# Summing the first half of the feed-forward shift on VectorE beside the output projection

## The chip, the cores and the metric

The kernel runs on one core of a Trainium2 chip. The metric is the device time of one execution in microseconds. The kernel before was run three times: 1297.34, 1301.3 and 1302.14 us, median 1301.3 us. Another execution was recorded by the hardware profiler; it took 1299.62 us, of which the profile's span covers 1297.8.

## The reference

One layer of a decoder with a batch of one, 256 tokens (T), width 2048 (D) and a feed-forward width of 5632, all in float32:

```python
cond = silu(c)
mod = (cond @ w_mod + b_mod).reshape(B, 6, D)
sh1, sc1, g1, sh2, sc2, g2 = [mod[:, i, None, :] for i in range(6)]
h = rmsnorm(x, norm_mix) * (1.0 + sc1) + sh1
proj = h @ w_in
...
y = concatenate([gla, gated_deltanet, pool, fox], -1) @ w_out
x = x + g1 * y
h = rmsnorm(x, norm_ffn) * (1.0 + sc2) + sh2
x = x + g2 * conv_ffn(h, w_gate, w_up, conv_w, conv_b, w_down)
return rmsnorm(x, norm_final)
```

The four mixers (gated linear attention, gated delta rule, pooling, forgetting attention) have 512 columns each. What the change concerns is `mod`: six vectors of 2048 numbers, each a product of the one vector `cond` with 2048 rows of `w_mod`. `sh2`, the shift ahead of the feed-forward part, is needed only after the output projection and the norm.

## The kernel before

**Stages.** By the trace: the input projection and the first two modulation vectors to about 240 us, then the rest of the input projection together with the four mixers, to about 448 us; the output projection to 541; the norm; the feed-forward part to the end. TensorE multiplies float32 weights as a sum of three products of rounded halves: ScalarE casts a loaded weight tile `wr` to its high half `wh`, VectorE takes the rest as `wl` (`load_split`, L158–163), and each k-row tile needs three matmuls of (`xh`,`wh`), (`xh`,`wl`), (`xl`,`wh`).

**The modulation gemvs.** The vectors that are needed later are made in halves of 1024 columns, in the background: a "job" is a letter and a half, `s0`, `s1` for the scale `sc2`, `h0`, `h1` for the shift `sh2`, `g0`, `g1` for the gate `g1`. A job (`gemv`, L171–206) goes through 16 rows of tiles of `w_mod`, two per step, each a transfer of 512 KB into a ring `wm` of four buffers, issued by SP. There are two ways to sum them.
- On TensorE (`ON_PE`): four matmuls of 32 columns by 512 for a row tile pair go side by side into four column strips of one PSUM bank `bgt`; at the end ScalarE copies the bank to a buffer `gr` of the `wr` ring, and eight matmuls with one column each (`sel`) add the strips and turn the row into a column, which VectorE adds to `s2` or `sh2` (`to_col`).
- On VectorE (`ON_DVE`): 16 scalar-tensor-tensor operations `ga <- wm, cond, ga` sum the rows within each partition; the end is matmuls with `ones`, eight of one column for a column vector (`to_col`) or two of 512 for a row (`to_row`, the `g` jobs).

**What sets the order.** The program is written as generators. While the last part of the input projection is emitted piece by piece, `paced` (L908) advances the two background streams by 0.38 and 0.69 of a step per piece; what is left of them is drained at L940–943. The `g` jobs wait with their end until the `s` jobs and the mixer whose buffer they reuse are emitted. A scheduler then orders the instructions of each engine by priority and by its own estimate of when each can run, so matmuls of one strand fill holes of another. Each engine works through its queue in that order; SP issues the transfers in its order too, and a transfer that waits for a buffer holds those behind it.

**The output projection.** `project(n, a)` (L952) goes through five chunks of columns (512, 512, 512, 256, 256) and, within one, through the 16 row tiles of `w_out` in the order of the mixers. A load is 512 KB: two row tiles of 512 columns or four of 256, so the chunks have 8, 8, 8, 4 and 4 loads. A load of two row tiles gives 12 matmuls of 512 columns (two row tiles, two halves of the tokens, three products), and chunk 0 has 96. Chunk 0 sums into the banks `ext`, chunk 1 into `oxt`, chunk 2 into `wot`, then `ext` and `oxt` again. Chunk 0 can run beside the end of the mixers as far as the mixers' results are there.

**The end of the mixers.** The delta rule (`gated_deltanet`) is a chain over four chunks of 64 tokens on banks `gdt`; its output is normed (`jk` squares on ScalarE, `oss` on VectorE and one power on POOL at L726, then `Y`), transposed (`gdt<-ident,Y`, L735) and multiplied into `pr`. The forgetting attention (`fox`) has four heads of two tiles: scores in `oxt` (last matmul `oxt<-ngr,idr`), maximum on VectorE (L868), exponent on ScalarE, reciprocal on VectorE (L870), scaling on ScalarE, one or two transposes (`oxt<-ident,p`, L873), a copy `pt` on ScalarE, and three matmuls with the values (`oxt<-pt,fv`). The results are split into the halves of `Y2` (in rows: `bigA<-pr`), which `project` multiplies. The tile `x1` (in rows `bigC`) takes x again for the residual sum, by two transfers of 1 MB (L979).

Of the kernel before, what the change touches and what calls it, by code (L numbers as in the profile page):

```python
# [49 lines left out]

ORDER = "gpfd"

ON_PE, PE_RATE = "s0 s1 h0", 0.38
ON_DVE, DVE_RATE = "h1 g0 g1", 0.69


def _consts():
# [16 lines left out]
def trunk_kernel(ctx: ExitStack, tc: tile.TileContext, x, c, w_mod, b_mod, norm_mix, norm_ffn, w_in,  # L74
# [21 lines left out]
    def mm(o, l, r, start=True, stop=True):  # L96
        PE.matmul(o, lhsT=l, rhs=r, start=start, stop=stop, skip_group_check=True)  # L97

    def tt(o, a, b, op):
        V.tensor_tensor(out=o, in0=a, in1=b, op=op)  # L100
# [10 lines left out]
    def act(o, a, f, **kw):  # L111
        S_.activation(o, a, f, **kw)

    def split(hi, lo, src):
        S_.copy(hi, src)  # L115
        tt(lo, src, hi.bitcast(F32), ALU.subtract)
# [36 lines left out]
    def load(view, k0, nk, c0, n):  # L153
        wr = wp.tile([P, 1024], F32, name="wr", tag="wr", bufs=5).rearrange("p (k n) -> p k n", n=n)
        nc.sync.dma_start(wr[:, 0:nk], view[:, k0:k0 + nk, c0:c0 + n])  # L155
        return wr

    def load_split(view, k0, nk, c0, n):  # L158
        wr = load(view, k0, nk, c0, n)
        wh = wp.tile([P, 1024], F32R, name="wh", tag="wh", bufs=3).rearrange("p (k n) -> p k n", n=n)  # L160
        wl = wp.tile([P, 1024], F32R, name="wl", tag="wl", bufs=3).rearrange("p (k n) -> p k n", n=n)
        split(wh[:, 0:nk], wl[:, 0:nk], wr[:, 0:nk])
        return wh, wl
# [51 lines left out]
    def to_col(dst, i, k0, nw, pst):  # L215
        def f(parts):
            b = pst()
            for j, (src, one) in enumerate(parts):
                for q in range(4):
                    mm(b[:, 4 * j + q:4 * j + q + 1], src[:, q * P:q * P + P], one[:, 0:1])  # L220
            o = dst[:, k0:k0 + 8]
            tt(o, b[:, 0:8], bm(i, k0, 8), ALU.add)
            if nw is not None:
                tt(o, o, nw[:, k0:k0 + 8], ALU.mult)
        return f


    with ExitStack() as ph:
# [16 lines left out]
        ext = lambda: exp_.tile([P, 512], F32, name="ext", tag="ext")  # L245
# [42 lines left out]
        with ExitStack() as st:  # L288
# [46 lines left out]
            def mods(g):  # L335
                for k0 in range(GROUPS[g][0], sum(GROUPS[g]), 4):
                    yield from mods4(k0, min(4, sum(GROUPS[g]) - k0))
# [135 lines left out]
                    yield from pair(p, done[p], g + 1)  # L473
                    done[p] = g + 1

            def jobs(seq, pst):
                col = pst or (ext)
                for job in seq.split():
                    kind, n = job[0], int(job[1])
                    k0, col0 = 8 * n, dict(s=4, h=3, g=2)[kind] * D + n * 1024  # L480
                    if kind == "s":
                        yield from gemv(col0, to_col(s2, 4, k0, nffn, col), pst)
                    elif kind == "h":
                        yield from gemv(col0, to_col(sh2, 3, k0, None, col), pst)
                    else:
                        yield from gemv(col0, g1_row(n, bgt), None,
                                        lambda: "gf"[n] in emitted and "s" in emitted, b_mod[:, col0:col0 + 1024])
# [3 lines left out]
            def marked(steps):  # L491
                yield from steps
                emitted.add("s")
# [4 lines left out]
            def g1_row(n, row):  # L498
                def f(parts):
                    name = ("gv", "fv")[n]  # L500
                    g1t[n] = cp.tile([P, 1024], F32, name=name, tag=name)
                    to_row(g1t[n], 0, row)(parts)
                return f

            bgt = lambda: bgp.tile([P, 512], F32, name="bgt", tag="bgt")
            bg = [marked(jobs(ON_PE, bgt)), jobs(ON_DVE, None)]
            for _ in mods(0):
                pass
            hold = [last_wm[0]]
# [437 lines left out]
        chunks = ((0, 512), (512, 512), (1024, 512), (1536, 256), (1792, 256))  # L947
        Y2 = bigA()

        def project(n, a):  # L950
            c0, w = chunks[n]
            nk = 1024 // w  # L952
            for j in range(KT // nk):
                ks = order[nk * j:nk * j + nk]
                if n == 0:
                    for k in ks:
                        split(Y2[:, k, 0:T], Y2[:, k, T:], pr[:, k + 4])
                wh, wl = load_split(wo_v, ks[0], nk, c0, w)
                steps = [(kk, k, t) for kk, k in enumerate(ks) for t in range(NT)]
                if n == len(chunks) - 1 and ks[-1] == order[-1]:  # L960

                    steps.sort(key=lambda s: s[2])
                for kk, k, t in steps:
                    st, sp_ = j + kk == 0, nk * j + kk == KT - 1
                    xh, xl = Y2[:, k, t * P:t * P + P], Y2[:, k, T + t * P:T + t * P + P]
                    mm(a[t], xh, wh[:, kk], start=st, stop=False)
                    mm(a[t], xh, wl[:, kk], start=False, stop=False)
                    mm(a[t], xl, wh[:, kk], start=False, stop=sp_)
# [3 lines left out]
        for n in range(2):  # L972
            project(n, sums[n])
# [7 lines left out]
        with tc.tile_pool(name="op", bufs=2, reuse_waits="tile") as op:  # L981
            for n, (c0, w) in enumerate(chunks):
                ns, gs = slice(c0, c0 + w), slice(c0 % 1024, c0 % 1024 + w)
                if n < 2:
                    a = sums[n]
                else:
                    a = [(wot, ext, oxt)[n - 2]()[:, 0:w] for _ in range(NT)]
                    project(n, a)
                for t in range(NT):
                    m_ = op.tile([P, 512], F32, name="m_", tag="m_")[:, 0:w]  # L990
                    tt(m_, a[t], g1t[c0 // 1024][:, gs], ALU.mult)
                    tt(x1[:, t, ns], x1[:, t, ns], m_, ALU.add)
                    act(m_, x1[:, t, ns], AF.Square, accum_out=x1s[:, t, n:n + 1])


    with ExitStack() as ph:
# [3 lines left out]
        with tc.tile_pool(name="hp", bufs=2, reuse_waits="tile") as hp:  # L1000
            s1 = hp.tile([P, 4], F32, name="s1", bufs=1)
# [145 lines left out]
```

## Time and profile before

| what | value |
|---|---|
| median of three runs | 1301.3 us (1297.34 to 1302.14) |
| profiled execution | 1299.62 us |
| its span in the profile | 1297.8 us |
| granted TensorE clock, mean | 0.985 |
| data moved over the span | 311.91 MB, mean 240 GB/s |
| matmuls `bgt<-wm,cond` (three jobs) | 192, 38.0 us busy |
| sums `ga<-wm,cond,ga` on VectorE | 139, 178.1 us busy, 1281 ns each |
| splits `wl<-wr,wh` on VectorE | 384, 469.4 us busy, 1223 ns each |

The profile is of one execution. It gives the busy time of each engine: PE is TensorE's matmuls, PEld its weight loads, DVE VectorE, ACT ScalarE, POOL GpSimd, SP the engine that issues the transfers. Rows of groups read: line, engine, operation, `out<-in`, shapes, count, then busy time, the mean of one in ns, and the idle time ahead of it with what ended that. Rows of the timeline begin with the start and the duration in us. PEclk is the TensorE clock that was granted, 1.00 being full speed. L97 is the line of a helper through which every matmul goes, so that groups are told apart by the names of tiles.

### The profile page before, as it was taken

Reading aid. Unit: us, or ns where it says so; the run is one execution under the profiler, and the core shown is the slowest. Engines: PE = TensorE matmul, PEld = TensorE weight load, DVE = VectorE, ACT = ScalarE, POOL = GpSimd, SP = SyncE. Lnnn points to the kernel's source line nnn. Section 1 sums busy time; section 2 is a strip of 40 time slices with the busy share of each in tenths; the row PEclk is TensorE's granted clock in tenths of the full one; section 3 lists DMA queues with packets and bytes.
Section 4 is the critical chain, followed back from the end, with each engine's and each line's share of the span. In section 5 each row is a group of like instructions: output and inputs, shape, how many; then the busy total and the mean of one; then the engine's idle time right before and its main releaser. Section 6 shows DMA issues by size and latency. Waiting matters only on the chain.

```text
span 1297.8 us, 19845 instructions
## 1 busy us (share of the span) xinstructions
PE 1243.1 (96%) x7663; PEld 1075.8 (83%) x7663; DVE 889.1 (69%) x1201; ACT 636.2 (49%) x1000; POOL 23.1 (2%) x31
## 2 busy tenths in 40 slices
PE   2799999999999999999999999999999999999995
PEld 1799999898876688888888888888888888888884
DVE  7679797989763397676657666665666587964543
ACT  3455344774354454564545545554545444443432
POOL 0200000010000100000000000000000000000000
PEclk9799999999999999999999999999999999999998
DMA  9899999796567898556576666657665699875552
GB/s 326 274 367 377 333 333 302 255 334 227 163 231 248 306 330 279 155 165 192 163 212 193 179 196 194 182 172 209 186 191 165 212 364 379 307 259 184 193 194 81
DMA packets 168597, 311.91 MB, mean 240 GB/s; under 512 B 16172, under 2 KB 54067, under 8 KB 167863
## 3 DMA queue, kind: packets, MB, share of 16 engines
q1 hardware_dynamic: 168503, 310.65, 73.0%
q8 instruction: 60, 0.98, 0.3%
q14 instruction: 34, 0.28, 0.1%
HBM read 308.51 MB, written 2.10 MB: 239 GB/s over the span
## 4 chain that ended last, share of the span: by engine, by line
PE 91%; DMA 4%; SPq 1%; DVE 1%; ACT 1%; issue 1%; POOLq 0%; ACTq 0%; DVEq 0%
PE fpt L97 57%; PE ext L97 16%; PE oxt L97 5%; PE acc L97 4%; PE gdt L97 4%; DMA wm<-in_w_mod_dram 3%; PE bgt L97 3%; PE wot L97 2%; DMA wr<-in_w_in_dram 1%; DVE ga L103 1%; ACT xT L1015 0%; SPq L155 0%; SPq L399 0%; DVE m L100 0%; DVE wl L100 0%
## 5 line engine op out<-in xcount | busy, mean ns | idle before, releaser
L100 DVE TENSOR_TENSOR wl<-wr,wh 128x1024 fp32r<-128x1024 f32 x384 | 469.4, 1223 | 293.7 <-ACT wh L115 292.9
L115 ACT CAST wh<-wr 128x1024 fp32r<-128x1024 f32 x384 | 403.6, 1051 | 489.5 <-PE fpt L97 316.5
L97 PE MATMUL fpt<-bigA,wh 128*128 128x512 f32 x1408 | 399.6, 396 | 2.1 <-DVE bigA L103 2.1
L97 PEld LDWEIGHTS fpt<-bigA,wh 128*128 128x128 f32 x1408 | 239.2, 189 | 32.9 <-issue 2.2
L97 PEld LDWEIGHTS fpt<-bigA,wl 128*128 128x128 f32 x1408 | 222.6, 188 | 34.2 <-DVE wl L100 3.7
L97 PE MATMUL fpt<-bigA,wl 128*128 128x256 f32 x1408 | 240.5, 279 | 0.0
L103 DVE SCALAR_TENSOR_TENSOR ga<-wm,cond,ga 128x1024 f32<-128x1024 f32 x139 | 178.1, 1281 | 11.5 <-DMA wm<-in_w_mod_dram 10.6
L97 PE MATMUL fpt<-wl,AH 128*128 128x512 f32 x352 | 137.5, 391 | 0.0
L97 PE MATMUL ext<-bigA,wh 128*128 128x256 f32 x768 | 137.3, 281 | 0.0
L97 PE MATMUL fpt<-wh,AL 128*128 128x512 f32 x352 | 137.0, 389 | 0.0
L97 PE MATMUL fpt<-wh,AH 128*128 128x512 f32 x352 | 123.5, 390 | 0.0
L97 PEld LDWEIGHTS ext<-bigA,wh 128*128 128x128 f32 x768 | 117.5, 189 | 3.0 <-DVE dS L100 0.8
L97 PE MATMUL ext<-bigA,wl 128*128 128x256 f32 x384 | 107.4, 280 | 1.7 <-DVE wl L100 1.7
L97 PE MATMUL ext<-wh,bigA 128*128 128x256 f32 (+1 forms) x384 | 79.3, 300 | 0.0
L97 PEld LDWEIGHTS fpt<-wh,AH 128*128 128x128 f32 x352 | 66.1, 188 | 14.1 <-ACT wh L115 0.2
L97 PEld LDWEIGHTS fpt<-wl,AH 128*128 128x128 f32 x352 | 66.1, 188 | 13.9 <-DVE m L100 0.2
L97 PEld LDWEIGHTS fpt<-wh,AL 128*128 128x128 f32 x352 | 66.1, 188 | 13.8 <-issue 0.2
L97 PE MATMUL acc<-bigA,wh 128*128 128x256 f32 x384 | 70.1, 289 | 4.6 <-ACT bigA L115 2.7
L97 PEld LDWEIGHTS ext<-bigA,wl 128*128 128x128 f32 x384 | 72.1, 188 | 2.8 <-DVE wl L100 1.9
L97 PEld LDWEIGHTS ext<-wh,bigA 128*128 128x128 f32 x384 | 61.6, 188 | 5.5 <-ACT wh L115 1.7
L97 PEld LDWEIGHTS acc<-bigA,wh 128*128 128x128 f32 x384 | 60.7, 199 | 5.0 <-ACT bigA L115 2.8
L97 PE MATMUL ext<-wl,bigA 128*128 128x256 f32 (+1 forms) x192 | 58.3, 304 | 1.6 <-DVE wl L100 1.6
(344 smaller groups left out, 1172.1 us busy)
## 6 DMA issues: line engine op xcount, KB each, us to landing
wm<-in_w_mod_dram SPq DMA_DIRECT2D x192, 512.0 KB, 5.7
wr<-in_w_in_dram SPq DMA_DIRECT2D x88, 512.0 KB, 9.1
wr<-in_ffn_w_gate_dram SPq DMA_DIRECT2D x88, 512.0 KB, 3.9
wr<-in_ffn_w_up_dram SPq DMA_DIRECT2D x88, 512.0 KB, 4.4
wr<-in_ffn_w_down_dram SPq DMA_DIRECT2D x88, 512.0 KB, 4.4
wr<-in_w_out_dram SPq DMA_DIRECT2D x32, 512.0 KB, 4.8
xt<-in_x_dram SPq DMA_DIRECT2D x2, 1024.0 KB, 7.1
bigC<-in_x_dram SPq DMA_DIRECT2D x2, 1024.0 KB, 12.2
```

The lines of the kernel that those rows point to most:

```text
L97: PE.matmul(o, lhsT=l, rhs=r, start=start, stop=stop, skip_group_check=True)
L100: V.tensor_tensor(out=o, in0=a, in1=b, op=op)
L103: V.scalar_tensor_tensor(out=o, in0=a, scalar=s, in1=b, op0=op0, op1=op1)
L115: S_.copy(hi, src)
```

## The change

`h0` leaves TensorE's list and becomes a stream of its own, `late`, summed on VectorE. It is advanced by one step (two rows of tiles, two transfers) at every third load of `w_out` from chunk 1 on, which gives eight steps at the loads 9, 12, … 30; what is left is drained behind the projection. Its end is eight matmuls with `ones` into the bank `bgt`. The pace of TensorE's stream rises from 0.38 to 0.48 of a step per piece, so its two jobs end earlier.

```diff
-ON_PE, PE_RATE = "s0 s1 h0", 0.38
+
+ON_PE, PE_RATE = "s0 s1", 0.48
 ON_DVE, DVE_RATE = "h1 g0 g1", 0.69
+LATE, LATE_LOADS = "h0", 3
...
-            def jobs(seq, pst):
-                col = pst or (ext)
+            def jobs(seq, pst, col=None):
+                col = col or pst or ext
...
             bg = [marked(jobs(ON_PE, bgt)), jobs(ON_DVE, None)]
+            late = jobs(LATE, None, bgt)
...
+        wo_loads = [0]
+
         def project(n, a):
...
                 wh, wl = load_split(wo_v, ks[0], nk, c0, w)
+                wo_loads[0] += 1
+                if n > 0 and wo_loads[0] % LATE_LOADS == 0:
+                    next(late, None)
...
+        for _ in late:
+            pass
```

The scheduler moves much besides. Line numbers after the change are higher by two to eleven (L97 becomes L99, L185 L187, L155 L157, L979 L987).

**TensorE at the end of the mixers.** Before, this is the order ahead of the last steps of the delta rule and behind them (`gdt` rows are the delta rule, `oxt` rows the attention, `bgt<-wm,cond` and `bgt<-sel,wr` the job h0):

```order
L97 MATMUL bgt<-wm,cond 32x512 x2
L97 MATMUL gdt<-X,bigC 64x128 x4
L97 MATMUL gdt<-bigC,dI 128x128 x4
L97 MATMUL gdt<-dS,bigC 64x128 x4
L97 MATMUL bgt<-sel,wr 128x1 x8
L97 MATMUL gdt<-bigC,dI 128x128 x4
L97 MATMUL gdt<-dS,bigC 64x128 x4
L97 MATMUL gdt<-X,bigC 64x128 x4
L873 MATMUL oxt<-ident,p 128x128
L97 MATMUL bgt<-ga,ones 128x512
L97 MATMUL oxt<-pr 128x256
L97 MATMUL oxt<-ct,la 128x256
```

The first projection matmul (`ext<-wh,bigA`) comes five rows further on, behind the transposes of `Y`, and from there on they stand between all steps of the last attention head. After the change, the corresponding place has no h0; it reads, from the last score matmul of the third head's second tile on:

```order
L99 MATMUL oxt<-ngr,idr 128x128
L99 MATMUL gdt<-bigC,dI 128x128 x4
L99 MATMUL gdt<-dS,bigC 64x128 x4
L99 MATMUL gdt<-X,bigC 64x128 x4
L876 MATMUL oxt<-ident,p 128x128 x2
L99 MATMUL oxt<-pt,fv 128x256
L99 MATMUL oxt<-pt,fv 128x128
L99 MATMUL oxt<-pr 128x128
L99 MATMUL oxt<-ct,la 128x128
L99 MATMUL oxt<-ngr,idr 128x128
L738 MATMUL gdt<-ident,Y 128x128 x4
L99 MATMUL ext<-wh,bigA 128x512
```

and goes straight on with:

```order
L99 MATMUL ext<-wl,bigA 128x512
L99 MATMUL ext<-wh,bigA 128x512
L99 MATMUL ext<-wl,bigA 128x512
L99 MATMUL ext<-wh,bigA 128x512 x2
L738 MATMUL gdt<-ident,Y 128x128 x4
L876 MATMUL oxt<-ident,p 128x128
L99 MATMUL oxt<-pr 128x256
L99 MATMUL oxt<-ct,la 128x256
L99 MATMUL oxt<-ct,la 128x128
L99 MATMUL oxt<-ngr,idr 128x128
L876 MATMUL oxt<-ident,p 128x128 x2
L99 MATMUL oxt<-pt,fv 128x256
```

Of chunk 0's 96 matmuls (`ext<-wh,bigA`, `ext<-wl,bigA`) 54 now stand ahead of the first of these rows, where h0's stood before and further up, 12 from some rows above them to the second `gdt<-ident,Y`, and 30 behind the last row; before, the whole 96 stood behind the delta rule's last matmul.

**VectorE in the same place.** Before, from the last tile's reciprocal on (`wl` are splits of `w_out`, `ga` the sums of g1, `bigA<-pr` the split of the mixers' results):

```order
L870 RECIPROCAL s_4571<-s_4571 128x1
L100 TENSOR_TENSOR oss<-oss,cq 128x4
L100 TENSOR_TENSOR wl<-wr,wh 128x1024 x2
L103 SCALAR_TENSOR_TENSOR pr<-gdt,V_74,pr 128x4x128
L100 TENSOR_TENSOR bigA<-pr,bigA 128x256 x4
L100 TENSOR_TENSOR wl<-wr,wh 128x1024
L103 SCALAR_TENSOR_TENSOR ga<-wm,cond,ga 128x1024
L100 TENSOR_TENSOR wl<-wr,wh 128x1024
L100 TENSOR_TENSOR bigA<-pr,bigA 128x256
L103 SCALAR_TENSOR_TENSOR ga<-wm,cond,ga 128x1024
```

After the change, from the reciprocal of the last head's first tile on (the second tile's follows at `s_4587`) to the first row of h0, which is the `TENSOR_SCALAR`:

```order
L873 RECIPROCAL s_4575<-s_4575 128x1
L105 SCALAR_TENSOR_TENSOR pr<-gdt,V_74,pr 128x4x128
L871 TENSOR_REDUCE s_4587<-oxt 128x1
L102 TENSOR_TENSOR bigA<-pr,bigA 128x256
L105 SCALAR_TENSOR_TENSOR ga<-wm,cond,ga 128x1024
L102 TENSOR_TENSOR bigA<-pr,bigA 128x256 x3
L873 RECIPROCAL s_4587<-s_4587 128x1
L105 SCALAR_TENSOR_TENSOR ga<-wm,cond,ga 128x1024 x3
L102 TENSOR_TENSOR bigA<-pr,bigA 128x256
L102 TENSOR_TENSOR wl<-wr,wh 128x1024 x2
L109 TENSOR_SCALAR ga<-wm,cond 128x1024
```

The sums of g1 began behind the mixers and now end there; h0's sums take the places beside the projection's splits which g1's had.

**SP's queue.** Before, its order of transfers from the series of `wm` on was:

```order
L185 DMA wm<-in_w_mod_dram 128x1024 x30
L155 DMA wr<-in_w_out_dram 128x2x512 x5
L979 DMA bigC<-in_x_dram 128x2048 x2
L155 DMA wr<-in_w_out_dram 128x2x512 x3
L180 DMA ga<-in_b_mod_dram 1x1024
L155 DMA wr<-in_w_out_dram 128x2x512 x3
L185 DMA wm<-in_w_mod_dram 128x1024
L155 DMA wr<-in_w_out_dram 128x2x512
L185 DMA wm<-in_w_mod_dram 128x1024
```

and after the change:

```order
L187 DMA wm<-in_w_mod_dram 128x1024
L157 DMA wr<-in_w_out_dram 128x2x512
L187 DMA wm<-in_w_mod_dram 128x1024 x2
L157 DMA wr<-in_w_out_dram 128x2x512
L187 DMA wm<-in_w_mod_dram 128x1024
L157 DMA wr<-in_w_out_dram 128x2x512
L187 DMA wm<-in_w_mod_dram 128x1024 x3
L157 DMA wr<-in_w_out_dram 128x2x512
L187 DMA wm<-in_w_mod_dram 128x1024
L987 DMA bigC<-in_x_dram 128x2048 x2
L187 DMA wm<-in_w_mod_dram 128x1024 x8
L157 DMA wr<-in_w_out_dram 128x2x512 x2
```

Thirteen loads of `w_out` now stand ahead of the reload of x (`bigC<-in_x_dram`) where five did, and eight `wm` between them. Behind the reload 20 `wm` follow up to the projection's last loads: the last four of g1, then the 16 of h0.

## The prediction

> **What bounds the kernel now.** The first view is the page itself: the busy shares, and the chain of work that ended last.
>
> ```profile
> PE 1243.1 (96%) x7663; PEld 1075.8 (83%) x7663; DVE 889.1 (69%) x1201; ACT 636.2 (49%) x1000; POOL 23.1 (2%) x31
> ...
> PE 91%; DMA 4%; SPq 1%; DVE 1%; ACT 1%; issue 1%; POOLq 0%; ACTq 0%; DVEq 0%
> PE fpt L97 57%; PE ext L97 16%; PE oxt L97 5%; PE acc L97 4%; PE gdt L97 4%; DMA wm<-in_w_mod_dram 3%; PE bgt L97 3%; PE wot L97 2%; DMA wr<-in_w_in_dram 1%; DVE ga L103 1%; ACT xT L1015 0%; SPq L155 0%; SPq L399 0%; DVE m L100 0%; DVE wl L100 0%
> ```
>
> TensorE (PE) is the bound over the whole span, and `bgt`, the bank in which the background gemvs are summed, stands in the chain itself. The next view is busy time in stretches of 20 us, from the attention's end to the first FFN matmuls (columns as in the second line of the answer).
>
> ```profile
> core 0: us, PE busy (x) PEld busy (x) DVE busy (x) ACT busy (x) POOL busy (x), PEclk, DMA share, GB/s
> 380.00:400.00 20.00, 19.53 (x122) 11.08 (x120) 9.72 (x28) 13.11 (x31) 0.00 (x0) 1.00 0.71 243
> 400.00:420.00 20.00, 20.00 (x138) 12.65 (x136) 8.28 (x23) 8.76 (x27) 0.00 (x0) 1.00 0.75 258
> 420.00:440.00 20.00, 20.00 (x131) 12.29 (x130) 6.13 (x18) 6.08 (x16) 0.00 (x0) 1.00 0.82 266
> 440.00:460.00 20.00, 20.00 (x117) 16.22 (x116) 9.45 (x20) 12.80 (x39) 3.76 (x3) 1.00 0.96 355
> 460.00:480.00 20.00, 20.00 (x90) 16.49 (x89) 19.52 (x23) 10.36 (x15) 0.00 (x0) 1.00 0.89 323
> 480.00:500.00 20.00, 20.00 (x89) 16.41 (x88) 19.46 (x19) 7.79 (x9) 0.00 (x0) 1.00 1.01 371
> 500.00:520.00 20.00, 20.00 (x92) 16.04 (x91) 13.16 (x14) 9.90 (x14) 0.96 (x1) 1.00 0.66 208
> 520.00:540.00 20.00, 20.00 (x172) 20.00 (x171) 10.95 (x13) 9.27 (x15) 0.00 (x0) 1.00 0.59 170
> ```
>
> TensorE has no hole from 400 to 540 us, while VectorE (DVE) is half idle to 460, full from 460 to 500 (there it does g1's sums beside the projection), and half idle again after. So work that leaves TensorE before 448 is worth its full length, if what is left still fills the engine.
>
> **What leaves TensorE.** The groups of `bgt`, and the eight matmuls that end a gemv summed on VectorE:
>
> ```profile
> L97 PE MATMUL bgt<-wm,cond 128*32 128x512 f32 x192 | 38.0, 603 | 1.1 <-DMA wm<-in_w_mod_dram 1.1
> L97 PE MATMUL bgt<-sel,wr 128*128 128x1 f32 x48 | 5.7, 249 | 0.0
> L97 PE MATMUL ext<-ones,ga 128*128 128x1 f32 x80 | 11.0, 268 | 13.0 <-DVE ga L103 13.0
> ```
>
> The 192 matmuls are three gemvs (s0, s1, h0); four stand side by side in four column strips, so the group's busy time counts, not 192 means. A third of 38.0 is 12.7 us, a third of the 48 column matmuls 1.9 us. Back come eight matmuls of the third row's kind: 11.0/80 × 8 = 1.1 us. **TensorE's work: −12.7 − 1.9 + 1.1 = −13.5 us.** The order shows s0 and s1 in slightly larger groups besides; worth 0 to 2 us, which I take at 0.
>
> **What fills the gap.** In before, h0's matmuls stand between the steps of the delta rule (gdn) and of the attention (fox), whose other half runs on DVE and ACT. In after the order of instructions puts chunk 0 of the projection there: counted in the order, 54 of its 96 matmuls stand ahead of the delta rule's last steps. Only 12 are left beside the tail, and 30 stand behind the last attention head. In before nearly all 96 lay beside the tail. The cover has been moved forward, and the tail's latencies come into the open. What they are, covered, in before's timeline:
>
> ```profile
> 447.54 0.31 PE L97 MATMUL oxt<-ngr,idr 128*128 128x128 f32 x1
> 450.35 0.42 DVE L868 TENSOR_REDUCE s<-oxt 128x1 f32<-128x256 f32 x1
> 450.81 0.48 ACT L112 ACTIVATE p<-oxt,s 128x256 f32<-128x256 f32 x1
> 452.55 0.16 DVE L870 RECIPROCAL s<-s 128x1 f32<-128x1 f32 x1
> 452.74 0.51 ACT L112 ACTIVATE p<-p,s 128x256 f32<-128x256 f32 x1 [1.37 <-DVE s L870]
> 456.33 0.38 PE L873 MATMUL oxt<-ident,p 128*128 128x128 f32 x2
> 457.11 0.51 ACT L875 COPY pt<-oxt 128x384 f32<-128x384 f32 x1
> 461.34 0.81 PE L97 MATMUL oxt<-pt,fv 128*128 128x256 f32 x4
> ```
>
> From the scores' end (447.85) to the transposes (456.33) a tile took 8.5 us, of which the chain itself is 0.42 + 0.48 + 0.16 + 0.51 = 1.6 us with hand-offs beside it (about 1.8); the rest is DVE and PE doing other things first. From the transposes' end to the end of the copy `pt`: 457.62 − 456.71 = 0.9 us.
>
> In after there are three such waits left once the delta rule is ending. VectorE's queue there holds g1's `ga` sums, which before did in the projection, and `wl` splits:
>
> ```profile
> 466.51 1.22 DVE L100 TENSOR_TENSOR wl<-wr,wh 128x1024 fp32r<-128x1024 f32 x1
> 467.64 1.28 DVE L103 SCALAR_TENSOR_TENSOR ga<-wm,cond,ga 128x1024 f32<-128x1024 f32 x1
> 468.84 1.22 DVE L100 TENSOR_TENSOR wl<-wr,wh 128x1024 fp32r<-128x1024 f32 x1
> 472.55 0.62 PE L97 MATMUL oxt<-wh,bigA 128*128 128x512 f32 x2
> 473.00 0.39 PE L97 MATMUL oxt<-wl,bigA 128*128 128x512 f32 x1
> 442.93 1.14 PE L97 MATMUL gdt<-bigC,dI 128*128 128x128 f32 x8
> ```
>
> I take a tile's wait at 1.8 us plus two `ga` of 1.28 ahead of its reduction or reciprocal, 4.4 us (bounds: 1.8 with nothing ahead, 8.5 as covered before). Against it stands what TensorE has between a tile's last score and its transposes. First tile: three groups of four delta-rule matmuls, 1.14/2 = 0.6 each, 1.7 us, so 2.7 us of idling. Second: two groups of four transposes of `Y` (0.6 each) and six chunk-0 matmuls at (473.00 − 472.55)/2 = 0.23, 2.6 us, so 1.8. Third: nothing at all, so 4.4. Two `pt` copies uncovered: 1.8. **Sum 10.7, taken as 10 us of idling**; with the bounds 1.8 and 8.5 it is 0.1 + 0 + 1.8 + 1.8 = 4 or 6.8 + 5.9 + 8.5 + 1.8 = 23.
>
> The delta rule's own end runs inside that stretch:
>
> ```profile
> 447.29 0.27 ACT L112 ACTIVATE jk<-gdt 128x128 f32<-128x128 f32 x1
> 451.65 1.85 POOL L726 TENSOR_TENSOR oss<-oss,mhalf 128x4 f32<-128x4 f32 x1 [7.45 <-DVE oss L109]
> 453.73 1.14 ACT L112 ACTIVATE Y<-gdt,oss 128x128 f32<-128x128 f32 x4 [0.48 <-DVE oss L100]
> ```
>
> Squares to normed `Y` took 454.87 − 447.29 = 7.6 us, 1.85 of it on POOL; before its last transposes TensorE has about 4.3 us of work in after (one p group, two of scores, six chunk-0 matmuls), 3.3 us short, against the 2.7 + 1.8 already counted up to the same point. It adds nothing to the sum but makes it firmer.
>
> **The rest of the change.** h0's 16 VectorE sums take g1's place beside the projection. In before a `wl` and a `ga` together take 468.84 − 466.51 = 2.33 us of VectorE, and the load they belong to 12 × 0.23 = 2.76 us of TensorE, which stayed at 20.00 of 20. That cover holds: 0. If it goes, VectorE sets the projection's pace; eight `m_`/`x1` operations and a few waits in the way would cost 0 to 3 us. The 16 `wm` transfers of h0 leave the long series that SP issued here:
>
> ```profile
> 381.50 56.94 SPq L185 DMA_DIRECT2D wm<-in_w_mod_dram  x30
> ```
>
> g1's 16 take their place, and h0's go to the projection, where g1's were; the stretches around it show 371 GB/s reached and the projection kept fed with g1's share: 0. The add to `sh2` stands ahead of chunk 3's additions in VectorE's order, well before the norm: 0. Earlier, TensorE takes s0 and s1 at a pace of 0.48 for 0.38 of a k-step per piece, so it may wait for `wm` more often. Three gemvs waited 1.1 us in all; I take 1.5 (0 to 3).
>
> **The sum:** −13.5 + 10 + 1.5 = −2 us. The profiled execution took 1299.62 us, 1297.8 of span and 1.8 around it; it gives 1297.6, so I say **1298 us**. The median of the three runs is 1301.3, so the same forecast is −0.25% by it. About 0.5%, 6.5 us, is what a measurement of this kernel can tell from no change: faster means below 1294.8, slower above 1307.8.
>
> Idling may also cost clock:
>
> ```profile
> 547.87 1.17 PE L97 MATMUL fpt<-bigA,wh 128*128 128x512 f32 x4 [2.07 <-DVE bigA L103]
> 548.00:550.00 2.00, 2.00 (x10) 1.73 (x11) 1.81 (x6) 0.91 (x2) 0.00 (x0) 0.83 0.04 8
> 550.00:552.00 2.00, 2.00 (x8) 1.72 (x8) 0.75 (x2) 0.67 (x1) 0.00 (x0) 0.50 0.00 0
> 552.00:554.00 2.00, 2.00 (x11) 1.69 (x11) 1.59 (x3) 1.19 (x3) 0.00 (x0) 0.82 0.00 0
> ```
>
> Behind the norm, where TensorE stood for 2.07 us after some shorter pauses, the granted clock was 0.83, 0.50 and 0.82 in the next three stretches of 2 us: 2 × (0.17 + 0.50 + 0.18) = 1.7 us lost by one such dip. The Trainium skill ("TensorE: Matmul & The Clock Gate", Part 1, What's actually happening) says that the clock goes to half after at least one idle window of about 3.4 us. By that rule waits as short as these cost no clock and the sum stays −2; by this trace, where no single pause was so long, one dip makes it −0.3. The forecast holds either way.
>
> **The rivals.**
> *The tail stays covered.* All engines' orders changed together, TensorE had no hole before, and my waits may be too long: with a wait of 1.8 us the idling is 4 us and nothing else is late. Then −13.5 + 4 = −9.5: **1290 us**; at best −13.5, 1286. For it: DVE at 6 to 10 of 20 up to 460 has room for g1. Against it: no matmul stands between the last tile's scores and its transposes.
> *The other side: VectorE's queue waits for a transfer.* In after the reload of x (two transfers, 2 MB) stands on SP ahead of g1's last four `wm`; VectorE's 13th `ga` of g1, which needs the first of these, stands ahead of the last tile's reciprocal.
>
> ```profile
> 445.61 0.82 SPq L979 DMA_DIRECT2D bigC<-in_x_dram  x2
> ...
> wm<-in_w_mod_dram SPq DMA_DIRECT2D x192, 512.0 KB, 5.7
> ...
> bigC<-in_x_dram SPq DMA_DIRECT2D x2, 1024.0 KB, 12.2
> ```
>
> In before the reload was issued at a buffer release during the tail, and took 12.2 us to land; nothing waited behind it. If in after the `wm` lands only 12 us (at worst 12.2 + 5.7 = 18) behind that release, the reciprocal comes as late, and TensorE, with at most 10 us of work and counted waits up to there, stands some 8 us more (18 − 10); with the clock dip and the projection at its dear end (+3) that is −2 + 8 + 1.7 + 3 = +10.7: **1310 us**. It decides for slower when that `wm` lands over 18 us after the release.
> *The projection becomes VectorE's.* +3 on the forecast, 1301; inside the same range.
>
> **How the numbers follow.** Forecast with its own range 1294 to 1305 (idling 7 to 17): 0.45. Covered tail: 0.35, nearly all below 1294.8. Queue behind the reload: 0.2, three quarters of it above 1307.8. So faster 0.38, same 0.45, slower 0.17. The range for 8 in 10 is 1286 (all of the 13.5 us) to 1309.
>
> **What the changed profile would show.** Right: `bgt<-wm` at 128 matmuls and about 25 us; PE short of 20.00 in the stretches before and during the last attention heads, by about 10 us, released by DVE or ACT; then 20.00 through the projection, with DVE full to about 510 us; chunk 0 ending at 471 or so instead of 472.5. Wrong, to the fast side: no hole there. To the slow side: DVE `ga` waiting on DMA `wm` in that stretch, with PE idle behind a reciprocal. The FFN should be unchanged; a difference there would speak against the whole working.

## The result, and the profile after

The changed kernel took **1310.2 us** in the median of five runs (1308.65 to 1315.38), the kernel before 1301.3. The ratio is 1.0077 with a 95% interval of 1.0059 to 1.0095: slower by about 9 us, where 1298 (1286 to 1309) had been forecast. The profiled execution took 1308.7 us with a span of 1306.9.

The page after the change, with the engines' busy time and the chain that ended last:

```profile
PE 1240.0 (95%) x7599; PEld 1077.6 (82%) x7599; DVE 908.0 (69%) x1217; ACT 636.4 (49%) x999; POOL 24.7 (2%) x31
...
PE 87%; DMA 6%; DVE 4%; ACT 1%; issue 1%; SPq 1%; POOLq 0%; ACTq 0%; DVEq 0%
```

TensorE has only 3.1 us less busy time and 12.2 us more idle time; together that is the 9.1 us by which the span grew. TensorE's share of the chain fell from 91% to 87%, VectorE's rose from 1% to 4%. The groups of the background bank after the change:

```profile
L99 PE MATMUL bgt<-wm,cond 128*32 128x512 f32 x128 | 25.4, 603 | 2.7 <-DMA wm<-in_w_mod_dram 2.7
...
L99 PE MATMUL bgt<-sel,wr 128*128 128x1 f32 x32 | 4.0, 255 | 0.0
...
L99 PE MATMUL bgt<-ones,ga 128*128 128x1 f32 x16 | 1.8, 245 | 0.0
```

So the work left TensorE as counted: 12.6 + 1.7 us gone, 1.8 added (a column job ends in 16 matmul records, not 8), **−12.5 us**. The rest of the change in busy time, +9.4 us, is the same matmuls counted longer: about 5.2 of it at half clock between 240 and 500 us and 2.2 ahead of 240 us; the remaining 2 us stay open. The windows show the stretches around the tail (the same view as before's; behind the span come the busy times of PE, PEld, DVE, ACT, POOL, then the granted clock, the DMA share and GB/s):

```profile
380.00:400.00 20.00, 20.00 (x155) 16.60 (x155) 16.62 (x33) 5.04 (x13) 0.00 (x0) 1.00 0.61 208
400.00:420.00 20.00, 17.27 (x117) 10.83 (x117) 8.93 (x24) 12.84 (x34) 0.00 (x0) 1.00 0.77 248
420.00:440.00 20.00, 20.00 (x100) 15.43 (x99) 14.54 (x20) 12.26 (x23) 0.95 (x1) 1.00 0.83 281
440.00:460.00 20.00, 17.18 (x115) 13.72 (x113) 17.91 (x32) 10.10 (x39) 3.94 (x2) 1.00 0.91 320
460.00:480.00 20.00, 14.08 (x46) 9.75 (x46) 10.18 (x14) 7.58 (x17) 0.00 (x0) 0.74 0.69 248
480.00:500.00 20.00, 20.00 (x90) 16.38 (x89) 19.51 (x20) 8.63 (x11) 0.00 (x0) 1.00 0.88 308
500.00:520.00 20.00, 20.00 (x89) 16.43 (x88) 19.67 (x20) 8.62 (x11) 0.00 (x0) 1.00 1.02 374
```

Where before stood at 20.00 throughout, TensorE now lacks 11.5 us between 400 and 480, and runs at a mean clock of 0.74 in the last of these stretches. Beside the projection (480 to 520) it is full although VectorE is, so h0's sums are covered there, as expected. Four rows of the same view, 2 us each, show the dip:

```profile
462.00:464.00 2.00, 0.29 (x4) 0.15 (x2) 0.76 (x2) 1.46 (x6) 0.00 (x0) 1.00 1.02 410
464.00:466.00 2.00, 0.00 (x0) 0.00 (x0) 1.69 (x3) 0.00 (x0) 0.00 (x0) 0.73 0.94 385
466.00:468.00 2.00, 0.69 (x2) 0.29 (x2) 1.96 (x5) 0.52 (x2) 0.00 (x0) 0.50 0.75 215
...
474.00:476.00 2.00, 2.00 (x8) 1.54 (x8) 0.00 (x0) 0.79 (x1) 0.00 (x0) 0.71 0.13 47
```

Between the last two rows lie three more stretches at 0.50, so the clock's loss in this dip is 2 × (0.27 + 4 × 0.50 + 0.29) = 5.1 us. That counts the half clock also while TensorE stood; weighed by its busy time the loss is 3.5 us. What TensorE waited for there, in the timeline of all engines (other rows left out):

```profile
461.99 0.31 PE L99 MATMUL oxt<-ngr,idr 128*128 128x128 f32 x1
462.33 0.42 DVE L871 TENSOR_REDUCE s<-oxt 128x1 f32<-128x256 f32 x1 [0.69 <-PE oxt L99]
462.90 0.47 ACT L114 ACTIVATE p<-oxt,s 128x256 f32<-128x256 f32 x1
464.31 1.28 DVE L105 SCALAR_TENSOR_TENSOR ga<-wm,cond,ga 128x1024 f32<-128x1024 f32 x1 [1.22 <-DMA wm<-in_w_mod_dram]
465.51 1.09 DVE L102 TENSOR_TENSOR bigA<-pr,bigA 128x256 fp32r<-128x256 f32 x3
466.51 0.15 DVE L873 RECIPROCAL s<-s 128x1 f32<-128x1 f32 x1
467.26 0.69 PE L876 MATMUL oxt<-ident,p 128*128 128x128 f32 x2 [4.97 <-ACT p L114]
```

This is the picture that the prediction drew for the slow side: the last tile's reciprocal stands behind a sum of g1, which waits 1.22 us for its `wm` behind the reload of x, and TensorE stands for 4.97 us. Whether it is also the cause had to be tried.

A second difference lies further up and was in no part of the forecast: two of the mixers begin later. The first matmuls of the linear attention's chunks, and the first transposes of the forgetting attention, in before:

```profile
305.35 0.43 PE L97 MATMUL oxt<-qE,E 64*128 64x64 f32 x2
...
398.74 0.33 PE L873 MATMUL oxt<-ident,p 128*128 128x128 f32 x1
```

and after the change:

```profile
318.57 0.43 PE L99 MATMUL oxt<-qE,E 64*128 64x64 f32 x2
...
412.14 0.27 PE L876 MATMUL oxt<-ident,p 128*128 128x128 f32 x1
```

Both stand 13 us later, before h0 has any part in it. And the whole loss is there when the projection's second chunk begins. Its first matmul came at 472.55 us in before, and the prediction expected it near 471; after the change it reads:

```profile
481.44 0.62 PE L99 MATMUL oxt<-wh,bigA 128*128 128x512 f32 x2
```

### The profile page after: what moved, and what is told of

It is laid out like the page before. It is cut to its first block, busy times and chain, and to the rows that moved or that the text cites. A ratio compares the mean times of both kernels' runs of the same rounds, so it can differ in the third digit from the quotient of the medians.

```text
span 1306.9 us, 19756 instructions
## 1 busy us (share of the span) xinstructions
PE 1240.0 (95%) x7599; PEld 1077.6 (82%) x7599; DVE 908.0 (69%) x1217; ACT 636.4 (49%) x999; POOL 24.7 (2%) x31
## 4 chain that ended last, share of the span: by engine, by line
PE 87%; DMA 6%; DVE 4%; ACT 1%; issue 1%; SPq 1%; POOLq 0%; ACTq 0%; DVEq 0%
PE fpt L99 56%; PE ext L99 15%; DMA wm<-in_w_mod_dram 5%; PE oxt L99 4%; PE acc L99 4%; PE gdt L99 3%; PE bgt L99 2%; PE wot L99 2%; DVE ga L105 2%; DMA wr<-in_w_in_dram 1%; DVE wl L102 0%; ACT xT L1026 0%; ACT wh L117 0%; DVE m L102 0%; SPq L157 0%
## 5 line engine op out<-in xcount | busy, mean ns | idle before, releaser
L99 PE MATMUL fpt<-bigA,wh 128*128 128x512 f32 x1408 | 399.5, 395 | 2.1 <-DVE bigA L105 2.1
L99 PEld LDWEIGHTS fpt<-bigA,wh 128*128 128x128 f32 x1408 | 239.2, 188 | 32.9 <-issue 2.2
L99 PEld LDWEIGHTS fpt<-bigA,wl 128*128 128x128 f32 x1408 | 222.5, 188 | 34.4 <-DVE wl L102 3.6
L99 PE MATMUL fpt<-bigA,wl 128*128 128x256 f32 x1408 | 240.4, 279 | 0.0
L105 DVE SCALAR_TENSOR_TENSOR ga<-wm,cond,ga 128x1024 f32<-128x1024 f32 x154 | 197.1, 1280 | 17.9 <-DMA wm<-in_w_mod_dram 15.9
L99 PE MATMUL ext<-bigA,wh 128*128 128x256 f32 x768 | 138.0, 281 | 0.0
L99 PE MATMUL fpt<-wl,AH 128*128 128x512 f32 x352 | 137.4, 390 | 0.0
L99 PE MATMUL fpt<-wh,AL 128*128 128x512 f32 x352 | 137.0, 389 | 0.0
L99 PE MATMUL fpt<-wh,AH 128*128 128x512 f32 x352 | 123.4, 390 | 0.0
L99 PEld LDWEIGHTS ext<-bigA,wh 128*128 128x128 f32 x768 | 117.4, 188 | 4.6 <-issue 1.9
L99 PE MATMUL ext<-bigA,wl 128*128 128x256 f32 x384 | 107.4, 280 | 2.0 <-DVE wl L102 2.0
L99 PE MATMUL ext<-wh,bigA 128*128 128x256 f32 (+1 forms) x384 | 82.6, 307 | 0.0
L99 PEld LDWEIGHTS fpt<-wh,AH 128*128 128x128 f32 x352 | 66.1, 188 | 14.1 <-ACT wh L117 0.2
L99 PEld LDWEIGHTS fpt<-wl,AH 128*128 128x128 f32 x352 | 66.1, 188 | 14.1 <-DVE m L102 0.2
L99 PEld LDWEIGHTS fpt<-wh,AL 128*128 128x128 f32 x352 | 66.1, 188 | 13.9 <-issue 0.2
L99 PEld LDWEIGHTS ext<-bigA,wl 128*128 128x128 f32 x384 | 72.2, 188 | 2.8 <-DVE wl L102 2.6
L99 PE MATMUL acc<-bigA,wh 128*128 128x256 f32 x384 | 70.2, 289 | 4.1 <-ACT bigA L117 2.8
L99 PEld LDWEIGHTS ext<-wh,bigA 128*128 128x128 f32 x384 | 62.2, 190 | 6.8 <-issue 3.5
L99 PEld LDWEIGHTS acc<-bigA,wh 128*128 128x128 f32 x384 | 60.3, 197 | 4.5 <-ACT bigA L117 2.9
L99 PE MATMUL ext<-wl,bigA 128*128 128x256 f32 (+1 forms) x192 | 58.8, 307 | 1.3 <-DVE wl L102 1.3
```

What stands on the lines that cost most here:

```text
L105: V.scalar_tensor_tensor(out=o, in0=a, scalar=s, in1=b, op0=op0, op1=op1)
```

## The experiments

The theory at the outset: the loss is made in the tail of the mixers, where TensorE has run out of work, VectorE's queue holds the last reciprocal, and idling costs clock. Rivals: h0's late sums and transfers; the pace of 0.48. Ratios are to the kernel before on the same chip, in 95% intervals.

**h0 left out.**

```diff
+    V.memset(sh2, 0.0)
-            late = jobs(LATE, None, bgt)
+            late = iter(())
```

> The changed kernel without h0 at all: its 16 VectorE sums, 16 transfers and the ends on TensorE and VectorE are left out, and the first half of the shift is zero (so the output lacks it). The order of TensorE up to the end of the mixers is the same. Tail theory (TensorE runs out of work at the end of the mixers, VectorE's queue and the reload of x hold the last reciprocal, the idling costs clock): the loss is all there, so 1304 to 1311 us, chunk 1 of the projection starting at 480 +- 2 us. Rival 'late work' (h0's sums and transfers beside the projection cost the 9 us): 1296 to 1300.

Measured 1311.8 us, ratio 1.0070 (1.0041 to 1.0099), just above the 1304 to 1311 of the tail theory; chunk 1 begins at 484.3, later than the 480 ± 2 expected and than the changed kernel's 481.4. Without any of h0's work the kernel is as slow. What h0 does beside the projection costs nothing that can be measured.

**The hole filled with useless matmuls.**

```diff
+                    if h == 3 and t == 1:
+                        bo = oxt()
+                        for i in range(4):
+                            mm(bo[0:32], s4[:, 1:2].to_broadcast([P, 32]), fv[:, i % 2, 0:512])
-                b = oxt()
+                b = bo if h == 3 else oxt()
```

> The changed kernel with four useless matmuls (32 columns, 512 wide, about 1 us each) between the scores of the last attention tile and its transposes, where TensorE stood for 5 us; the order is the same otherwise, and they are overwritten. If the hole costs clock (TensorE at half from 464 to 475 us, some 5 us lost): the dip goes or shrinks and the time falls by 2 to 5 us, 1305 to 1308. If the clock loss comes from elsewhere or is none: 1309 to 1312.

Measured 1315.7 us, ratio 1.0096 (1.0064 to 1.0129), in two groups of runs near 1309 and 1316, and above both ranges. Its window and rows of its timeline:

```profile
460.00:480.00 20.00, 15.89 (x67) 9.96 (x66) 11.30 (x19) 8.55 (x23) 1.55 (x1) 1.00 0.79 281
```

```profile
464.73 0.31 PE L99 MATMUL oxt<-ngr,idr 128*128 128x128 f32 x1
466.26 3.62 PE L99 MATMUL oxt<-fv,s 128*32 128x512 f32 x8 [1.23 <-ACT p L114]
470.84 0.44 PE L880 MATMUL oxt<-ident,p 128*128 128x128 f32 x2 [0.96 <-ACT p L114]
```

The dip in that stretch is gone, 1.00 for 0.74, as expected; the time is not lower. The transposes came 6.1 us behind the scores (470.84 − 464.73) where after had 5.3. The useless work did not hold them: TensorE waited 0.96 us more for `p` behind it, and on VectorE the sum ahead of the reciprocal waited 2.05 us for its `wm` instead of 1.22. That the dip alone made the loss is not supported; why the runs fall in two groups is open. It is also one execution: a dip can stay away with the pauses unchanged, as the last section shows.

**The reload of x behind g1's transfers.**

```diff
+        g1_last = last_wm[0]
...
-        for t in range(NT):
-            nc.sync.dma_start(x1[:, t], x_v[:, t])
+        with tc.issue_after(g1_last.ins):
+            for t in range(NT):
+                nc.sync.dma_start(x1[:, t], x_v[:, t])
```

> The changed kernel with the reload of x issued behind the last transfer of g1 instead of ahead of its last four. Tail theory with the reload as one part: no wait of ga for wm in the tail (1.2 us in after), the hole ahead of the last transposes 2.5 to 4 us instead of 5.0, 1304 to 1309 us; since the scheduler then also puts more sums of g1 ahead of the delta rule's last products on VectorE, at worst 1311. Rival 'late work': 1310, unchanged.

Measured 1309.9 us, ratio 1.0072 (1.0049 to 1.0095), not clear of the rival's 1310 and within the tail theory only by its worst case. Two of TensorE's waits from 240 to 490 us (us in total, times, longest), and the first row of TensorE's timeline behind the last scores, which end at 468.37:

```profile
PE bgt L99 <- DVE ga L105: 3.7, 1, 3.7
PE oxt L876 <- ACT p L114: 1.9, 2, 1.7
```

```profile
472.03 2.08 PE L99 MATMUL bgt<-ga,ones 128*128 128x512 f32 x2 [3.66 <-DVE ga L105]
```

The wait of `ga` for `wm` ahead of the last reciprocal is gone, but the hole in that place is still 3.7 us long, for 5.0: two matmuls of g1's row stand there ahead of the last transposes and wait for VectorE. (The 1.7 us are those of the third head, and the changed kernel has them too.) The reload is not the cause: its wait is one of several that stand behind each other.

**The pace, with h0 late.** The changed kernel with the pace of the kernel before, and two more:

```diff
-ON_PE, PE_RATE = "s0 s1", 0.48
+ON_PE, PE_RATE = "s0 s1", 0.38
```

> The changed kernel with the pace of TensorE's background stream back at 0.38. The order then has 25 matmuls of chunk 0 between the second and the third attention head and 12 ahead of the delta rule's end where after has 6. Tail theory: less idling, 1301 to 1307 us. If the pace has no part: 1309 to 1312.

Measured 1302.5 us, ratio 1.0011 (0.9996 to 1.0027). **The pace makes nearly the whole of the loss**: 1310.2 − 1302.5 = 7.7 of 9 us. And with the pace undone, moving h0 changes nothing that can be measured.

> The changed kernel with TensorE's background pace at 0.30. If the loss is the mixers' later start, the time falls on with the pace: first attention transposes before 400 us, chunk 1 at 468 to 473 us, 1293 to 1300. If 0.38 has already got all that the pace can give and the tail's own latencies bind: 1300 to 1304.

0.30 gave 1311.7 us, ratio 1.0087 (1.0059 to 1.0114), above both ranges: the time does not fall on with the pace. The attention's first transposes come at 407.4 us there, late again.

> The changed kernel at a pace of 0.43. If the pace pushes the mixers back in proportion: between 1302.5 (0.38) and 1310.2 (0.48), 1304 to 1309, first attention transposes between 400 and 412 us. If the order jumps: outside that, either way, with idling plus clock dips that account for the difference to 1302.5 within 3 us.

0.43 gave 1306.7 us, ratio 1.0043 (1.0023 to 1.0062), with the attention's first transposes at 401.1, hardly later than the 400.3 at 0.38. Both numbers lie in the ranges for a push in proportion, but the start has not moved with the time: a later start is not what costs there.

**The pace, with h0 on TensorE as before.**

```diff
-ON_PE, PE_RATE = "s0 s1 h0", 0.38
+ON_PE, PE_RATE = "s0 s1 h0", 0.48
```

> The kernel before with the pace alone changed, 0.48 for 0.38 (h0 stays on TensorE). Theory 'late start and no cover' (the pace pushes the mixers' start back by some 13 us, which costs only where TensorE has nothing else to do): the mixers start 8 to 15 us later here too; h0's matmuls stand in the tail, all 96 of chunk 0 behind the last head, so TensorE idles a few us more than before: 1302 to 1308. Rival 'the pace alone' (the late start costs its whole length): 1309 to 1313. If the pace is harmless: 1299 to 1303.

> The kernel before with the pace alone changed the other way, 0.30 for 0.38. If what costs is that any other pace deals the scheduler another order, one in which TensorE's cover lies elsewhere than the mixers' waits: idling and clock dips between 300 and 500 us, 1305 to 1318. If a fast pace costs only because it pushes the mixers back: 1296 to 1302.

0.48 gave 1317.6 us, ratio 1.0128 (1.0105 to 1.0152), and 0.30 gave 1318.8, ratio 1.0140 (1.0108 to 1.0172). Either way from 0.38 the kernel before loses 16 to 18 us, more than any of the theories allowed for 0.48, and just above the 1305 to 1318 expected for 0.30 if another order is what costs. The same work on TensorE, in one window from 240 to 500 us, for before:

```profile
240.00:500.00 260.00, 258.92 (x1813) 208.33 (x1813) 189.34 (x310) 134.15 (x281) 10.50 (x7) 1.00 0.78 269
```

at 0.48:

```profile
240.00:500.00 260.00, 248.60 (x1745) 199.05 (x1744) 181.68 (x303) 129.51 (x279) 9.76 (x7) 0.97 0.75 257
```

at 0.30:

```profile
240.00:500.00 260.00, 248.93 (x1744) 198.52 (x1743) 176.53 (x306) 130.38 (x277) 9.65 (x7) 0.97 0.73 249
```

and for the changed kernel, whose TensorE has 12.5 us less to do:

```profile
240.00:500.00 260.00, 244.73 (x1687) 200.23 (x1686) 196.31 (x312) 130.46 (x276) 11.70 (x7) 0.97 0.75 253
```

Idle time is 1.1, 11.4 and 11.1 us with h0 on TensorE, and the clock adds 6.8 us in the last two (1 − granted clock, summed over windows of 2 us). With h0 on VectorE at 0.48 the kernel is 7.4 us faster than with h0 on TensorE at 0.48 (1310.2 against 1317.6): the move, with the orders that come with it, does pay where the order is poor anyway.

**h0 left out at the pace of 0.38.** The edits of the first experiment and of the fourth.

> The changed kernel without h0 (first half of the shift zero) and with the pace at 0.38. h0's late work costs nothing at 0.48, so here too: 1299 to 1304, like 0.38 with it, although TensorE has some 14 us less to do than before. If h0's late work does cost where the tail is shorter: 1292 to 1298.

Measured 1299.6 us, ratio 0.9990 (0.9979 to 1.0001). With 14.3 us of work taken off TensorE and put nowhere, the kernel gains about 2 us (2.7 at most, by the interval). Its window, and that of pace 0.38 with h0 late:

```profile
240.00:500.00 260.00, 252.54 (x1730) 206.96 (x1729) 191.57 (x310) 135.21 (x286) 10.66 (x8) 0.98 0.70 236
```

```profile
240.00:500.00 260.00, 251.78 (x1732) 206.77 (x1731) 204.60 (x321) 133.89 (x283) 9.71 (x7) 0.98 0.78 265
```

The mixers begin when they did in before (linear attention 305.4, forgetting attention 398.4), but the last transposes come at 460.2 for 456.3, and chunk 1 at 473.6 for 472.6. In place of the 14.3 us, idle time and half clock have grown by 11.5 (7.5 + 5.1 − 1.1).

**Sums out of the tail.** Pace 0.38, g1 moved to the late stream, each step's transfers held behind a load of `w_out`:

```diff
-ON_DVE, DVE_RATE = "h1 g0 g1", 0.69
-LATE, LATE_LOADS = "h0", 3
+ON_DVE, DVE_RATE = "h1 g0", 0.69
+LATE, LATE_LOADS = "g1 h0", 1
...
-                if n > 0 and wo_loads[0] % LATE_LOADS == 0:
-                    next(late, None)
+                if wo_loads[0] in (6, 8, 10, 12, 14, 16, 18, 20) or wo_loads[0] > 21:
+                    with tc.issue_after(last_wr[0].ins):
+                        next(late, None)
```

> Pace 0.38, and the late stream made of g1 and then h0, each step's transfers held behind a load of w_out from the sixth on, so that VectorE has few sums left in the tail and TensorE keeps chunk 0 spread through it. Theory 'VectorE's sums in the tail hold the mixers' chain': chunk 1 starts 3 to 8 us before that of pace 0.38 (474.8), and the whole gains as much unless VectorE then binds the projection: 1294 to 1300. Theory 'only the mixers' start counts': 1301 to 1304.

Measured 1309.9 us, ratio 1.0074 (1.0057 to 1.0090). Chunk 1 began at 473.7, so the tail is only 1 us shorter than at 474.8, where 3 to 8 had been expected, and the time lies above both ranges; the loss came behind it:

```profile
500.00:560.00 60.00, 51.10 (x329) 46.45 (x328) 48.52 (x59) 26.40 (x44) 1.65 (x2) 0.91 0.81 293
```

TensorE stood 8.9 us and lost 5.1 by the clock there (before 2.7 and 1.7); the matmuls that end h0 waited 7.1 us for its sums. Then with the steps at the loads 5, 6, 8, 9, 11, 12, … 21, and 22 to 25, so that h0 ends earlier:

> As the held stream at pace 0.38 (chunk 1 at 473.7 us, but 8.9 us of idling and 5.1 us of clock behind 500 us), with the steps of g1 and h0 set so that h0 ends some seven loads before the projection does. If the late end of the shift was what cost there: the idling behind 500 us is back at 2.7 us, 1299 to 1304. If VectorE's queue in the projection is the bound: 1305 to 1311.

1299.5 us, ratio 0.9996 (0.9978 to 1.0014): the loss behind the projection is gone (2.3 and 1.7 us), so it was the late shift. It is the best of the versions that compute the whole, and equal to the kernel before within what can be measured.

**The chain of heads.** The fourth head of the attention left out, in the kernel before and at pace 0.38 with h0 late (`for h in range(3)`):

> The kernel before with the fourth head of the forgetting attention left out (its queries go on in place of its result). It is about 4 us of TensorE's work. Theory 'the attention's chain of heads bounds the pace-0.38 kernel without h0's matmuls, TensorE's work bounds the kernel before': here only the work goes, chunk 1 starts 3 to 6 us earlier than 472.6, 1295 to 1299. Rival 'the chain bounds the kernel before too': 8 to 15 us earlier, 1287 to 1293.

> The changed kernel at pace 0.38 with the fourth head left out in the same way. Chain theory: the last head's latency goes with it, and most of the idling: chunk 1 starts 9 to 16 us earlier than 474.8, 1286 to 1294, and less than the kernel before without it by 3 us or more. If TensorE's work binds here too: 3 to 6 us, 1296 to 1300, equal to the kernel before without it.

1296.6 (0.9956, 0.9936 to 0.9976) and 1296.8 us (0.9955, 0.9941 to 0.9969): both gain the work of a head and no more. The theory that the last head's latency bounds the kernel without h0 falls by the time. Chunk 1 did begin 13 us earlier in the second, at 461.8, as that theory asked, but this is ahead of the last transposes of `Y` (467.0), and the end did not follow. What remains of its idle time between 400 and 500 us (4.8 us, and 3.4 by the clock) is spread: 2.0 us are waits of the delta rule's matmuls, whose last `gdt<-X,bigC` came at 460.9, and 1.3 us the third head's transposes.

**The attention ahead of the pooling** (`ORDER = "gfpd"`), in before, at pace 0.38, and at pace 0.38 with g1 and h0 held at the loads 5 to 12 and 14 to 28:

> The kernel before with the attention ahead of the pooling (the order of mixers g, f, p, d instead of g, p, f, d), nothing else. TensorE has no hole in before, so an earlier attention gains nothing there: 1298 to 1305.

> The changed kernel at pace 0.38 with the attention ahead of the pooling. Chain theory: the attention starts and ends some 8 to 12 us earlier, and chunk 0 then fills TensorE behind it: chunk 1 starts at 462 to 469 us, 1289 to 1297, faster than both kernels. If the work or VectorE's queue binds: 1299 to 1304.

> Pace 0.38, attention ahead of pooling, and the late stream made of g1 (one step at each of the loads 5 to 12, held behind that load) and h0 (at the loads 14 to 28). With the attention earlier, the delta rule ended last and VectorE was full from 430 to 470 us. If VectorE's sums held it there: idling 400 to 500 us at most 4 us instead of 7.6, chunk 1 at 464 to 470 us, 1293 to 1299. If the delta rule's own latencies bind: 1300 to 1305.

1305.7 (1.0029, 1.0016 to 1.0041), 1301.9 (1.0003, 0.9990 to 1.0017) and 1302.9 us (1.0018, 1.0005 to 1.0032). The attention's last transposes move to 441.9 from 461.5, but the delta rule's transposes of `Y` stay where they were (463.5 for 462.0), and TensorE idles 7.6 us between 400 and 500 us all the same; its longest waits there, 2.5 and 2.0 us, are for ScalarE's casts of `wh` and `bigA`. Taking g1's sums from there changed the idle time little (7.5 us). At pace 0.38 the two chains end together, and moving one forward leaves the other.

**The account.** For each kernel, over 240 to 500 us: TensorE's work against before, its idle time, and the clock's loss (the sum of 1 − granted clock over windows of 2 us), less before's 1.1 us; beside it the time of the same execution less before's 1299.62, and the difference of the medians.

| kernel | work | idle | clock | sum less 1.1 | same execution | medians |
|---|---|---|---|---|---|---|
| after (0.48, h0 late) | −12.5 | 15.3 | 6.8 | +8.5 | +9.1 | +8.9 |
| 0.38, h0 late | −12.5 | 8.2 | 5.1 | −0.3 | +1.4 | +1.2 |
| 0.30, h0 late | −12.5 | 14.8 | 12.0 | +13.2 | +10.2 | +10.2 |
| 0.43, h0 late | −12.5 | 9.1 | 6.8 | +2.3 | +4.5 | +5.9 |
| before, 0.48 | 0 | 11.4 | 6.8 | +17.1 | +18.7 | +16.1 |
| before, 0.30 | 0 | 11.1 | 6.8 | +16.8 | +18.0 | +18.0 |
| 0.38, no h0 | −14.3 | 7.5 | 5.1 | −2.8 | +0.2 | −1.9 |
| held, in time | −12.5 | 7.0 | 3.4 | −3.2 | −1.1 | −1.3 |
| 0.48, no h0 | −14.3 | 13.2 | 11.9 | +9.7 | +10.5 | +10.6 |
| 0.48, hole filled (3.6 us more work) | −8.9 | 12.7 | 3.4 | +6.1 | +9.2 | +14.4 |
| 0.48, reload behind | −12.5 | 13.4 | 13.6 | +13.4 | +12.7 | +8.7 |

The sums agree with the same executions within some 3 us, and with the medians within 5, but for the filled hole, whose median lies in its higher group. The clock column counts half clock also where TensorE stands and loses nothing by it; weighed by busy time it is 5.2 for 6.8 in the first row, 9.5 for 12.0 at 0.30, and at most 1.3 less in the others. All this is bookkeeping: it says that the time was lost by TensorE standing, or running at half clock, between 240 and 500 us, and not why an order leaves it so.

## Why the prediction was wrong

- **What leaves TensorE** was right: −13.5 forecast, −12.5 measured. The 16 records of a column job for 8 make most of the difference.
- **The step that failed is the pace.** The prediction put 0.48 for 0.38 at 1.5 us, as more waiting for `wm`. That waiting did come out so (2.7 us for 1.1). But the pace also dealt the scheduler another order: between 244 us and the input projection's last matmul TensorE has 328 matmuls in the delta rule's banks instead of 264 (43.5 us busy instead of 33.8), and that last matmul comes at 399.8 instead of 380.2 us. The linear and the forgetting attention then begin 13 us later. That goes with the loss, but the runs do not show that it makes it: at 0.43 the kernel loses 4 us against 0.38 without such a late start. By the pace alone the changed kernel loses 7.7 us, and the kernel before 16. The prediction compared the orders only from the tail on.
- **The tail** was right in kind: the cover is gone and the waits come into the open. At the old pace, where only h0's move is left, TensorE idles 6.2 us between 400 and 500 us, against 10 forecast, and loses 5.1 by the clock, where the sum had nothing. That the two together, 11.3, come near 10 is luck. So h0's move gains nothing: −12.5 + 12.2 (with the small idle times from 240 us on) is the measured no change. The range would have held that kernel's 1302.5.
- **The slow rival** named 1310 us, and its pieces are in the trace: the `ga` that waits for `wm` behind the reload, and a reciprocal behind it. But the run without that wait took the same time, and the rival's own condition did not hold: it asked for a `wm` that lands over 18 us behind the buffer's release, and the sum waited for it only to 464.31, 10.5 us behind the reload's issue at 453.85. The number agrees, the reason does not.
- **The covered tail** (1290) needed TensorE's holes to stay filled; none of the runs with h0 off TensorE shows it.
- **The projection** carried h0's sums at little or no cost, as forecast: the kernel without h0 is not faster at 0.48, and by 3 us at 0.38 (1299.6 against 1302.5; the intervals of the ratios overlap barely), of which 1.8 us are the matmuls that end h0.
- **The clock** was weighed at one dip of 1.7 us that would not matter. It was 6.8 us in all, about half as much as the added idle time of 14.2. The Trainium skill ("TensorE: Matmul & The Clock Gate", Part 1, What's actually happening) has half clock after at least one idle window of about 3.4 us. The trace agrees in part: the stop of 4.97 us brought a dip, but the clock fell 2.6 us into it, and the other dip of the changed kernel came without a pause ahead of it (last section).

What stays open: by which of its rules the scheduler comes to the orders at 0.30 and 0.48, which feature of these orders costs the time, and why the 0.38 of the kernel before is full; that was not tried beyond these paces.

## What to carry to other kernels

An engine that is busy without a hole is not therefore the bound: part of its work may be cover for chains on the other engines, and work taken from there turns into idle time. The test is to leave the work out altogether: here that gained about 2 us of 14. And where one number sets the order in which a scheduler sees the work, a change that retunes it is two changes; try them apart, and compare the orders along the whole stretch, not only where the edit's own instructions stand.

## What the runs showed of the hardware

The clock's losses come in pieces. Summed over a stage, they were 1.7, 3.4, 5.1, 6.8, 12.0 and 13.6 us, that is 1 to 4, 7 and 8 times 1.7: half clock for whole pieces of about 3.4 us. This agrees with the window of about 3.4 us that the Trainium skill names ("TensorE: Matmul & The Clock Gate", Part 1, What's actually happening). In the changed kernel TensorE stopped at 462.3, the clock fell near 464.9, and it was whole again near 475.2, some 8 us after work came back at 467.3 with small gaps. With the hole filled by matmuls of 32 columns, and no wait over 1.7 us, it stayed at 1.00.

Pauses alone do not tell whether a piece is lost. In the changed kernel the clock was at half from 335.2 to 338.6 us, with no pause from 310 us on:

```profile
310.00:334.00 24.00, 24.00 (x195) 20.12 (x193) 17.68 (x25) 10.87 (x18) 0.00 (x0) 1.00 0.59 190
334.00:336.00 2.00, 2.00 (x16) 2.00 (x17) 0.93 (x1) 1.12 (x3) 0.00 (x0) 0.80 1.06 377
336.00:338.00 2.00, 2.00 (x11) 2.00 (x11) 1.97 (x8) 1.33 (x2) 0.00 (x0) 0.50 1.10 385
```

And at the norm, where the pauses of 0.60 and 2.07 us went with a dip in the kernel before, the run with the hole filled had pauses of 0.59 and 2.07 us and none:

```profile
558.19 1.17 PE L99 MATMUL fpt<-bigA,wh 128*128 128x512 f32 x4 [2.07 <-DVE bigA L105]
...
500.00:600.00 100.00, 97.33 (x603) 86.86 (x602) 73.63 (x103) 53.62 (x83) 1.65 (x2) 1.00 0.66 212
```

So a dip that comes or stays away in one execution is weak evidence for a cause.
